# Gate matrices from two float32r products per token, with the gate split into a high and a low part

## The chip, the cores and the metric

The kernel runs on one core of a Trainium2 chip. The metric is device time in microseconds (us), the median of several executions. A core has five engines that run their own instruction queues in order: TensorE (PE, matrix products; its weight loads are shown apart as PEld), VectorE (DVE), ScalarE (ACT), GpSimd (POOL) and SyncE (SP, which only issues transfers here). PE writes its results to a small memory of its own, PSUM, from where DVE or ACT read them.

## What is computed

One residual block over 1024 tokens of width 1024: a normalisation, one input projection, mLSTM heads and gated MLP heads (the "mixers"), an output projection, and then PEER, a layer that picks 16 of 16384 single-neuron experts for each of 8 heads and each token. This last part matters here:

```
s    = scores of a token's query against 2 x 128 keys, per head
s1, i1 = top 16 of the first 128;  s2, i2 = top 16 of the second 128
top_s, pos = top 16 of the 256 sums s1 + s2      -> expert i1 * 128 + i2
gate = softmax(top_s)                            (16 per head, 128 per token)
a    = gelu(x . expert_u[expert])
out  = sum over the token's 128 picks of a * gate * expert_v[expert]
```

## The kernel before

The 1024 tokens are eight blocks of 128. Five blocks (0 to 4) are "dense": all 16384 experts are multiplied out for them, and a gate matrix that is zero for the experts not picked weighs the result. Three blocks (5 to 7) are "sparse": their picked experts are gathered row by row.

The front runs in three parts, with blocks 0 and 1, blocks 2 to 4, and blocks 5 to 7. Each part loads and normalises its tokens, runs the mixers (`head`, `group`), the output projection (products named `po`) and the queries with their scores (`query`: products `pq` and `psc`). Most products there are float32r (`F32R`), three for each pair of matrices, each matrix split into a high and a low part (`mm3`, L94 to L96). After the front come the experts (`experts`): products `pa` and `pout`, while POOL gathers rows for the sparse blocks.

For each dense block, top-k work on DVE (`topk_units`) yields for every token its 128 picks as three rows: first key index, second key index and gate. `done` transposes the three with PE (L483), so that a token is a column, and ACT copies the result to the tile `ijgT` (L485).

`gate_units` then builds the gate matrices in 32 quads of four tokens per block, 160 in all. A token's 128x128 matrix, indexed by the two key indices, is a product of two one-hot matrices over its 128 picks, one of which carries the gates. In a quad, DVE compares a row of the numbers 0 to 127 with both indices of four tokens in one operation (L653, tile `AB`); ACT multiplies one of the one-hots of each token by its gates (L656); PE makes one F32 product per token (L658, tile `pG` in PSUM); ACT copies the four matrices out, transposed, to `Gt` (L659). Every eighth quad a 2 MB piece goes to memory (`d_G`, L661), from where the experts read it (`Gin`, L768). Three buffers of `AB` and two of `pG` bound how many quads are in flight.

The order of instructions on each engine is fixed when the program is built, by a scheduler that follows the program's order. The gate and top-k work of one part's dense blocks is handed out among the next part's work: `interleave` calls the next of these pieces as the main work's given costs (28 for a head, 12 for a group, and so on) add up, and all of them are handed out by a total of 210 out of some 330. So the quads of blocks 0 and 1 stand in the second part's mixers and output projection, and those of blocks 2 to 4 in the third part's. The sparse part has no quads. Operations under `self.first()` (PSUM evictions of the main work) take precedence in that order.

Of the kernel before, what the change touches and what calls it, by code (L numbers as in the profile page):

```python
# [7 lines left out]
F32 = mybir.dt.float32  # L8
F32R = mybir.dt.float32r
# [3 lines left out]
AF = mybir.ActivationFunctionType  # L13
OP = mybir.AluOpType
# [23 lines left out]
NAB = 3  # L38
# [8 lines left out]
class Build:  # L47
# [402 lines left out]
    def topk_units(self, blk):  # L450
        nc, v, tk = self.nc, self.nc.vector, self.tk
# [26 lines left out]
        def done():  # L478
            ijg = st["ijg"]
            if blk in self.dense:  # L480
                pt = self.gps.tile([128, 3, 128], F32, name="pG", tag="pG", bufs=2)
                for k in range(3):
                    nc.tensor.transpose(pt[:, k], ijg[:, k], self.ident)  # L483
                t = self.gp.tile([128, 3, 128], F32, name="ijgT", tag="ijgT", bufs=1)
                nc.scalar.activation(t, pt, AF.Copy)  # L485
                self.pick[blk] = t

        L = []
        for h0 in range(0, 8, HB):
# [149 lines left out]
    def gate_units(self, blk):  # L639
        nc = self.nc  # L640
        pool = self.gp
        s = self.dense.index(blk)
        st = {}

        def quad(tt, q):
            t3 = self.pick[blk]
            if q == 0:
                st["G"] = pool.tile([128, NEXP, TG], F32, name="Gt", tag="Gt", bufs=2)
            Gt = st["G"]
            pg = self.gps.tile([128, 4, 128], F32, name="pG", tag="pG", bufs=2)  # L650
            AB = pool.tile([128, 2, 4, 128], F32, name="AB", tag="AB", bufs=NAB)
            t0 = tt * TG + q * 4
            nc.vector.tensor_tensor(AB, self.iota[:, None, None, :].to_broadcast([128, 2, 4, 128]),  # L653
                                    t3[:, 0:2, t0:t0 + 4, None].to_broadcast([128, 2, 4, 128]), op=OP.is_equal)
            for u in range(4):
                nc.scalar.activation(AB[:, 1, u], AB[:, 1, u], AF.Copy, scale=t3[:, 2, t0 + u:t0 + u + 1])  # L656
            for u in range(4):
                nc.tensor.matmul(pg[:, u], AB[:, 1, u], AB[:, 0, u], start=True, stop=True)  # L658
            nc.scalar.activation(Gt[:, :, q * 4:q * 4 + 4], pg.rearrange("p q i -> p i q"), AF.Copy)  # L659
            if q == TG // 4 - 1:  # L660
                nc.scalar.dma_start(self.d_G[s * (128 // TG) + tt], Gt)  # L661

        return [lambda tt=tt, q=q: quad(tt, q) for tt in range(128 // TG) for q in range(TG // 4)]

    def row(self, pool):

        self.nrow += 1
        if self.dense_phase and self.nrow % (NAB + NGAT) < NAB:
            return self.gp.tile([128, D], F32, name="gat", tag="AB", bufs=NAB)
        return pool.tile([128, D], F32, name="gat", tag="gat", bufs=NGAT)  # L670
# [325 lines left out]
```

## Time and profile before

| | |
|---|---|
| time, median of 3 runs | 2878.07 us (2872.08 to 2878.95) |
| the profiled execution's own time | 2855.23 us |
| its span, first to last instruction | 2853.5 us |
| busy: PE, DVE, POOL, ACT | 94%, 77%, 54%, 39% of the span |
| mean granted clock of TensorE | 0.977 of 2.4 GHz |

The profile is of one execution. "Busy" is the time in which an engine worked on an instruction. A row of a group names the line of the kernel, the engine, the operation, what it writes and reads, its shape (partitions x elements) and how often it ran, and behind the bar the busy time in us, the mean duration of one in ns, and how long the engine stood idle just before, with what ended that. float32r operands of a matrix product are shown as f32. The chain of waits is the work that ended last, followed back from the end to what released each step.

### The profile page before, as it was taken

To read this page: it belongs to the slowest core of one execution; us is meant where nothing else is said; L and a number is where in the kernel's file an instruction comes from. 1 tells how busy PE (TensorE), PEld (TensorE's weight loads), DVE (VectorE), ACT (ScalarE), POOL (GpSimd) and SP (SyncE) were. 2 spreads that over 40 slices of the span, in tenths; PEclk is the share of its full clock that TensorE was granted. 3 is DMA by queue.
4 is the path that set the end of the run, shared out by engine and by line. 5 is a ranking of instruction groups with operands and counts; after the bars stand their busy time and mean duration, and the time that the engine had idled before them with its cause. 6 is when DMAs were issued, how large, how long until landed. Compare 5 with 4: busy or idle time off the path is not lost.

```text
span 2853.5 us, 44691 instructions
## 1 busy us (share of the span) xinstructions
PE 2687.1 (94%) x16223; PEld 2457.0 (86%) x16223; DVE 2195.5 (77%) x4979; ACT 1119.8 (39%) x2293; POOL 1529.3 (54%) x1256
## 2 busy tenths in 40 slices
PE   7888999899899799999999999999999999999998
PEld 6787988889789798889888898889888899889987
DVE  6638985189985777888898788978987777777774
ACT  5444798347888432222222232223222222222222
POOL 4531120001100187767767687767767777777873
PEclk9899999999999899999999999999999999999999
DMA  7788657875669798989989999898889999999992
GB/s 262 238 304 298 228 192 288 275 251 204 228 234 308 278 326 308 325 307 330 332 290 336 339 329 331 309 346 309 316 283 326 356 324 330 346 328 325 338 338 98
DMA packets 329278, 842.63 MB, mean 295 GB/s; under 512 B 25929, under 2 KB 161505, under 8 KB 317281
## 3 DMA queue, kind: packets, MB, share of 16 engines
q0 software_dynamic: 115456, 432.07, 41.2%
q1 hardware_dynamic: 190544, 347.91, 36.8%
q10 hardware_dynamic: 23056, 59.81, 5.5%
q8 instruction: 127, 2.08, 0.3%
q14 instruction: 95, 0.77, 0.1%
HBM read 750.52 MB, written 89.16 MB: 294 GB/s over the span
## 4 chain that ended last, share of the span: by engine, by line
PE 56%; DVE 20%; DMA 10%; issue 5%; ACT 5%; POOL 3%; SPq 1%; ACTq 0%; POOLq 0%; DVEq 0%
PE pout L94 7%; PE pout L96 7%; PE pa L96 7%; PE pout L95 7%; PE pa L94 7%; PE pa L95 7%; PE pG L658 3%; DVE gat L694 2%; DMA Gin<-d_G 2%; DVE sacc L710 2%; DMA gat<-v,ix 2%; DVE AB L653 2%; PE pq L94 2%; PE pq L96 2%; PE pq L95 2%
## 5 line engine op out<-in xcount | busy, mean ns | idle before, releaser
L94 PE MATMUL pa<-xh,uhi 128*128 128x320 f32 x2048 | 637.0, 311 | 24.5 <-ACT uhi L775 14.1
L95 PE MATMUL pa<-xl,uhi 128*128 128x320 f32 x2048 | 634.8, 310 | 0.0
L96 PE MATMUL pa<-xh,ulo 128*128 128x320 f32 x2048 | 623.5, 310 | 4.0 <-POOL ulo L776 3.7
L710 DVE SCALAR_TENSOR_TENSOR sacc<-gat,aw,sacc 128x1024 f32<-128x1024 f32 x384 | 492.1, 1282 | 38.4 <-DMA gat<-v,ix 35.8
L94 PE MATMUL pout<-vhi,wh 128*128 128x512 f32 x1280 | 502.9, 398 | 19.4 <-ACT wh L787 9.8
L95 PE MATMUL pout<-vlo,wh 128*128 128x512 f32 x1280 | 506.5, 397 | 0.4 <-POOL vlo L799 0.4
L96 PE MATMUL pout<-vhi,wl 128*128 128x512 f32 x1280 | 489.3, 397 | 0.7 <-DVE wl L788 0.7
L706 POOL DMA_INDIRECT gat<-v,ix x384 | 364.6, 950 | 228.5 <-DVE sacc L710 126.2
L690 POOL DMA_INDIRECT gat<-u,ix x384 | 364.7, 950 | 200.5 <-DVE gat L694 106.3
L694 DVE SCALAR_TENSOR_TENSOR gat<-gat,xn 128x1024 f32<-128x1024 f32 x384 | 459.0, 1212 | 16.8 <-DMA gat<-u,ix 16.7
L94 PEld LDWEIGHTS pa<-xh,uhi 128*128 128x128 f32 x2048 | 387.4, 189 | 38.1 <-DVE wl L788 14.7
L96 PEld LDWEIGHTS pa<-xh,ulo 128*128 128x128 f32 x2048 | 383.8, 189 | 11.7 <-POOL ulo L776 7.2
L95 PEld LDWEIGHTS pa<-xl,uhi 128*128 128x128 f32 x2048 | 387.3, 189 | 7.3
L776 POOL TENSOR_TENSOR ulo<-raw,uhi 128x1024 fp32r<-128x1024 f32 x128 | 308.8, 2414 | 140.3 <-ACT uhi L775 138.3
L798 ACT ACTIVATE vhi<-raw 128x1024 fp32r<-128x1024 f32 x128 | 131.7, 1052 | 508.7 <-PE pout L95 414.1
L799 POOL TENSOR_TENSOR vlo<-raw,vhi 128x1024 fp32r<-128x1024 f32 x128 | 308.2, 2418 | 26.0 <-ACT vhi L798 24.5
L813 DVE TENSOR_TENSOR acc<-acc,pout 128x512 f32<-128x512 f32 x320 | 214.2, 682 | 124.5 <-PE pout L96 124.2
L94 PEld LDWEIGHTS pout<-vhi,wh 128*128 128x128 f32 x1280 | 240.6, 188 | 73.6 <-DVE acc L813 12.5
L96 PEld LDWEIGHTS pout<-vhi,wl 128*128 128x128 f32 x1280 | 240.2, 189 | 54.8 <-DVE wl L788 1.6
L95 PEld LDWEIGHTS pout<-vlo,wh 128*128 128x128 f32 x1280 | 241.6, 189 | 50.7 <-POOL vlo L799 0.8
L787 ACT ACTIVATE wh<-pa 128x320 fp32r<-128x320 f32 x256 | 111.8, 437 | 358.9 <-DVE pa L786 358.7
L786 DVE TENSOR_TENSOR pa<-pa,Gin 128x320 f32<-128x320 f32 x256 | 126.6, 494 | 154.0 <-ACT pa L784 115.4
(238 smaller groups left out, 5036.9 us busy)
## 6 DMA issues: line engine op xcount, KB each, us to landing
raw<-uT SPq DMA_DIRECT2D x128, 512.0 KB, 6.0
raw<-v SPq DMA_DIRECT2D x128, 512.0 KB, 4.5
wlo<-d_wl SPq DMA_DIRECT2D x48, 1024.0 KB, 5.6
d_G<-Gt ACTq DMA_DIRECT2D x20, 2048.0 KB, 12.0
Gin<-d_G SPq DMA_DIRECT2D x32, 1280.0 KB, 14.3
wraw<-win SPq DMA_DIRECT2D x72, 512.0 KB, 6.9
d_wl<-wlo POOLq DMA_DIRECT2D x24, 1024.0 KB, 8.8
wraw<-wq SPq DMA_DIRECT2D x48, 512.0 KB, 7.5
```

The costliest lines, as they stand in the source:

```text
L94: te.matmul(ps, lh, rh, start=k == 0, stop=False)
L95: te.matmul(ps, lh, rl, start=False, stop=False)
L96: te.matmul(ps, ll, rh, start=False, stop=k == n - 1)
L690: gd = nc.gpsimd.indirect_dma_start(out=t, out_offset=None, in_=self.I["u"], in_offset=bass.IndirectOffsetOnAxis(ap=st["ix"][:, k:k + 1], ...
L694: v.scalar_tensor_tensor(t, t, 1.0, st["xn"], op0=OP.mult, op1=OP.mult, accum_out=st["a"][:, k:k + 1])
L706: gd = nc.gpsimd.indirect_dma_start(out=t, out_offset=None, in_=self.I["v"], in_offset=bass.IndirectOffsetOnAxis(ap=st["ix"][:, k:k + 1], ...
L710: v.scalar_tensor_tensor(st["acc"], t, st["a"][:, k:k + 1], st["acc"], op0=OP.mult, op1=OP.add)
L776: nc.gpsimd.tensor_tensor(ul, ur, uh.bitcast(F32), op=OP.subtract)
L786: v.tensor_tensor(p3, p3, G[:, s * (n32 // 2):(s + 1) * (n32 // 2), e], op=OP.mult)
L798: nc.scalar.activation(vh, vr, AF.Copy)
L799: nc.gpsimd.tensor_tensor(vl, vr, vh.bitcast(F32), op=OP.subtract)
L813: v.tensor_add(st["acc"][:, s, dl], st["acc"][:, s, dl], po)
```

## The change

The gates of a block are split once, in `done`: a high part `ghi`, rounded to float32r by ACT, and a low part, held as its ratio to the high part (`glo`), by four small DVE operations. In a quad, DVE compares only the first index for four tokens (tile `B`, a new tile in the front's memory pool with three buffers). For each token one more DVE operation compares the second index and multiplies by the high gate, and ACT multiplies its result by the ratio, which gives the low part. Both one-hots are now float32r, and PE adds two float32r products per token, high and low, where it made one F32 product.

```diff
@@ topk_units: done @@
                 t = self.gp.tile([128, 3, 128], F32, name="ijgT", tag="ijgT", bufs=1)
                 nc.scalar.activation(t, pt, AF.Copy)
-                self.pick[blk] = t
+                gh = self.gp.tile([128, 128], F32R, name="ghi", tag="ghi", bufs=1)
+                gl = self.gp.tile([128, 128], F32, name="glo", tag="glo", bufs=1)
+                nc.scalar.activation(gh, pt[:, 2], AF.Copy)
+
+                v.tensor_sub(gl, t[:, 2], gh.bitcast(F32))
+                v.tensor_single_scalar(t[:, 2], gh.bitcast(F32), 1e-30, op=OP.max)
+                v.reciprocal(t[:, 2], t[:, 2])
+                v.tensor_mul(gl, gl, t[:, 2])
+                self.pick[blk] = (t, gh.bitcast(F32), gl)
@@ gate_units: quad @@
-            AB = pool.tile([128, 2, 4, 128], F32, name="AB", tag="AB", bufs=NAB)
+            AB = pool.tile([128, 2, 4, 128], F32R, name="AB", tag="AB", bufs=NAB)
+            B = self.fp.tile([128, 4, 128], F32R, name="B", tag="B", bufs=NAB)
             t0 = tt * TG + q * 4
-            nc.vector.tensor_tensor(AB, self.iota[:, None, None, :].to_broadcast([128, 2, 4, 128]),
-                                    t3[:, 0:2, t0:t0 + 4, None].to_broadcast([128, 2, 4, 128]), op=OP.is_equal)
+            nc.vector.tensor_tensor(B, self.iota[:, None, :].to_broadcast([128, 4, 128]),
+                                    t3[:, 0, t0:t0 + 4, None].to_broadcast([128, 4, 128]), op=OP.is_equal)
             for u in range(4):
-                nc.scalar.activation(AB[:, 1, u], AB[:, 1, u], AF.Copy, scale=t3[:, 2, t0 + u:t0 + u + 1])
+                t = t0 + u
+                nc.vector.tensor_scalar(AB[:, 0, u], self.iota, t3[:, 1, t:t + 1], gh[:, t:t + 1],
+                                        op0=OP.is_equal, op1=OP.mult)
+                nc.scalar.activation(AB[:, 1, u], AB[:, 0, u].bitcast(F32), AF.Copy, scale=gl[:, t:t + 1])
             for u in range(4):
-                nc.tensor.matmul(pg[:, u], AB[:, 1, u], AB[:, 0, u], start=True, stop=True)
+                for k in range(2):
+                    nc.tensor.matmul(pg[:, u], AB[:, k, u], B[:, u], start=k == 0, stop=k == 1)
```

## Rows read from the trace of the kernel before

**Rows 1.** The page: its span, the busy time of each engine with its share of the span and its instructions, and the shares of the lines in the chain of waits.

```profile
span 2853.5 us, 44691 instructions
PE 2687.1 (94%) x16223; PEld 2457.0 (86%) x16223; DVE 2195.5 (77%) x4979; ACT 1119.8 (39%) x2293; POOL 1529.3 (54%) x1256
PE pout L94 7%; PE pout L96 7%; PE pa L96 7%; PE pout L95 7%; PE pa L94 7%; PE pa L95 7%; PE pG L658 3%; DVE gat L694 2%; DMA Gin<-d_G 2%; DVE sacc L710 2%; DMA gat<-v,ix 2%; DVE AB L653 2%; PE pq L94 2%; PE pq L96 2%; PE pq L95 2%
```

**Rows 2.** Busy time of each engine by stage: the stretch, its length, then us of PE, PEld, DVE, ACT and POOL with the number of instructions, the granted clock, and the share and rate of the transfers.

```profile
315.00:430.00 115.00, 106.09 (x836) 101.94 (x834) 104.29 (x287) 101.97 (x285) 22.33 (x26) 1.00 0.56 201
430.00:490.00 60.00, 57.62 (x484) 56.33 (x483) 36.48 (x49) 53.03 (x141) 5.01 (x8) 1.00 0.76 280
490.00:660.00 170.00, 151.98 (x954) 142.54 (x953) 93.40 (x470) 77.49 (x135) 10.44 (x21) 0.96 0.76 262
660.00:820.00 160.00, 142.53 (x1064) 135.89 (x1063) 153.47 (x554) 130.43 (x350) 23.34 (x30) 0.96 0.56 201
820.00:950.00 130.00, 124.28 (x924) 122.98 (x923) 78.40 (x160) 110.63 (x292) 2.86 (x6) 0.99 0.89 314
...
985.00:2853.00 1868.00, 1818.31 (x9984) 1630.90 (x9984) 1489.79 (x2565) 486.83 (x804) 1352.38 (x1040) 0.99 0.90 317
```

**Rows 3.** The same stretches, for the one-hots of the gate quads alone (L653): us of DVE, with the number of instructions.

```profile
315.00:430.00 115.00, 53.00 (x43) 1.00 0.56 201
430.00:490.00 60.00, 26.83 (x21) 1.00 0.76 280
...
660.00:820.00 160.00, 62.12 (x51) 0.96 0.56 201
820.00:950.00 130.00, 55.03 (x46) 0.99 0.89 314
```

**Rows 4.** The chain of waits in 315 to 490 us and in 660 to 950 us: shares of the stretch by engine and line.

```profile
by line: PE pG L658 16.5%; DVE AB L653 15.2%; ACT AB L656 7.9%; PE po L94 6.2%; PE po L96 6.1%; PE po L95 5.9%; DVE cv L287 3.4%; PE pg L94 3.1%; PE pg L96 3.1%; PE pg L95 3.1%; ACT Gt L659 2.9%; issue 1.7%; ACT L399 1.5%; ACT whi L77 1.3%;
...
by line: PE pG L658 15.1%; DVE AB L653 9.3%; ACT AB L656 5.5%; SPq L745 4.4%; DMA kk<-keys 4.0%; PE po L94 3.2%; PE pq L96 3.1%; PE pq L94 3.1%; PE po L95 3.1%; PE po L96 3.1%; PE pq L95 3.0%; DMA xl<-d_xl 2.7%; DMA scb<-d_sc 2.1%; ACT Gt L
```

**Rows 5.** Who waited for whom, in 315 to 490 us and in 660 to 950 us: us in total, how often, the longest.

```profile
DVE AB L653 <- PE pG L658: 11.0, 13, 2.9
...
DVE AB L653 <- PE pG L658: 29.4, 21, 5.6
```

**Rows 6.** Groups of instructions of the gate quads.

```profile
L653 DVE TENSOR_TENSOR AB<-iota,ijgT 128x1024 f32<-128x1024 f32 x160 | 197.0, 1240 | 56.0 <-PE pG L658 40.4 <-ACT sc L443 5.7 <-ACT AB L656 5.2
L658 PE MATMUL pG<-AB 128*128 128x128 f32 x1280 | 183.7, 281 | 16.5 <-ACT AB L656 10.7 <-ACT Gt L659 5.4
...
L659 ACT ACTIVATE Gt<-pG 128x512 f32<-128x512 f32 x160 | 92.4, 586 | 20.1 <-PE pG L658 19.3
```

**Rows 7.** DVE in order of time, from three places: start in us, duration in us (of several in a row, from the first start to the last end), then engine, line, operation, tiles, shape and count.

```profile
345.60 1.21 DVE L653 TENSOR_TENSOR AB<-iota,ijgT 128x1024 f32<-128x1024 f32 x1
346.73 0.54 DVE L291 SCALAR_TENSOR_TENSOR qk<-zz,cv 128x384 f32<-128x384 f32 x1
...
347.27 0.46 DVE L285 TENSOR_SCALAR cv<-zz,convw,convb 128x384 f32<-128x384 f32 x1
347.66 0.28 DVE L551 MAX8 tv<-s 128x8 f32<-128x128 f32 x1
...
404.70 0.86 DVE L405 TENSOR_SCALAR vv<-gu,mv,grr 128x128 f32<-128x128 f32 x3 [1.08 <-POOL grr L63]
```

**Rows 8.** Groups of DVE instructions that are near the added ones in form; the last is an answer for one line, with durations in ns as least, median and most.

```profile
L341 DVE TENSOR_TENSOR wT<-pS,wT 128x128 f32<-128x128 f32 x21 | 5.8, 277 | 0.0
...
L151 DVE TENSOR_SCALAR diag<-ident,rall 128x128 f32<-128x128 f32 x6 | 1.7, 286 | 4.2 <-POOL rall L63 4.2
...
L540 DVE RECIPROCAL gsum<-gsum 128x4 f32<-128x4 f32 x8 | 1.3, 161 | 0.0
...
L813 DVE TENSOR_TENSOR acc<-acc,pout x320: 650/682/690, 1029.5 to 2841.7; 128x512 f32<-128x512 f32 x160
```

**Rows 9.** PE in order of time, from four places: the first products after PE had stood, a quad's gate products, and float32r products of 512 and 320 columns.

```profile
321.63 0.39 PE L94 MATMUL pvo<-whi,ah 128*128 128x256 f32 x1 [0.21 <-DVE zz L282]
...
321.85 0.28 PE L95 MATMUL pvo<-wlo,ah 128*128 128x256 f32 x1
...
321.97 0.29 PE L96 MATMUL pvo<-whi,al 128*128 128x256 f32 x1
...
461.49 1.05 PE L658 MATMUL pG<-AB 128*128 128x128 f32 x8
...
1999.82 0.63 PE L96 MATMUL pout<-vhi,wl 128*128 128x512 f32 x2
...
2000.87 0.31 PE L94 MATMUL pa<-xh,uhi 128*128 128x320 f32 x1
2001.01 0.31 PE L95 MATMUL pa<-xl,uhi 128*128 128x320 f32 x1
```

**Rows 10.** ACT in order of time: a quad's four scalings.

```profile
461.46 1.28 ACT L656 ACTIVATE AB<-AB,ijgT 128x128 f32<-128x128 f32 x4
```

**Rows 11.** The transfers of the gate matrices: their issues (durations of the issue in ns, first and last start in us), and the time to landing of all of them.

```profile
L768 SPq DMA_DIRECT2D Gin<-d_G x32: 377/377/426, 978.1 to 2763.1; - x32
L661 ACTq DMA_DIRECT2D d_G<-Gt x20: 326/327/359, 343.0 to 950.3; - x20
...
DMA to landing us min/median/max: 11.1/13.2/20.7
```

More of the change, by code (lines that the diff above doesn't have):

```diff
@@ L645, in quad @@
         def quad(tt, q):
-            t3 = self.pick[blk]
+            t3, gh, gl = self.pick[blk]
             if q == 0:
```

## The prediction

> **What bounds the kernel now.** I read the page first: TensorE (PE) is busy for 94% of the span, VectorE (DVE) for 77%, and by lines the chain of waits is mostly expert products; the gate product, L658, has 3% of it and its one-hots, L653, 2% [rows 1]. These are averages over unlike stages, so next come the busy times stage by stage [rows 2] and, in the same stretches, those of the gate one-hots alone [rows 3]. The 160 quads of gate work (four tokens each) lie in 315 to 490 and 660 to 950 us and nowhere else: the four stretches hold 161, one of them counted on both sides of a border. The 1868 us of experts hold none, and I take their length as unchanged.
>
> There are two kinds of gate stretch. In the mixers (315 to 430, 660 to 820) DVE works 104.3 of 115 and 153.5 of 160 us, more than PE or about as much: DVE sets the pace, PE and ScalarE (ACT) close behind. Behind the mixers (430 to 490, 820 to 950) PE works 57.6 of 60 and 124.3 of 130 us, ACT 53.0 and 110.6, DVE only 36.5 and 78.4: PE sets it. The chain agrees: in both halves L658 and L653 are its two largest lines, 16.5% and 15.2%, then 15.1% and 9.3% [rows 4]. The waits inside the gate work are small beside this: L653 waits for a buffer that L658 frees for 11.0 and 29.4 us in all, mostly where DVE has time [rows 5]. So the change is priced in the mixers on DVE and behind them on PE.
>
> **Prices now.** Durations on DVE overlap: L653 at 345.60 us takes 1.21, but the next operation starts 1.13 later [rows 7]. The step from start to start is what counts; it is some 0.08 us shorter than the duration. Thus L653 costs DVE 1.13 us a quad. On PE a quad is eight records (an F32 product is two, hence 1280 for 640 tokens [rows 6]) in 1.05 us, the last one 0.275 long: a step of 0.111, or 0.89 us a quad [rows 9]. On ACT it is four scalings in 1.28 us, a step of 0.30, and one copy of some 0.48 [rows 6, 10].
>
> **The change on DVE.** The 1024-wide comparison goes; a 512-wide one (B) and four 128-wide compare-and-multiply operations with two per-partition scalars come.
> - B: the 512-wide two-source row L813 has 682 ns, so a step of 0.60 [rows 8].
> - Compare-and-multiply: the trace has neither this pair of operations nor its float32r output, but L405 is a 128-wide F32 operation with two such scalars. Three of them take 0.86 us, the last one 0.34: a step of 0.26 [rows 7]. From below, L151 with one scalar has 286 ns, a step of 0.21 [rows 8]; from above, I let it cost no more than the 384-wide two-scalar L285, whose next operation starts 0.39 later [rows 7]. I take 0.26, the nearest form.
> - A quad then costs 0.60 + 4 x 0.26 = 1.64 us, 0.51 more than now; 0.31 more (1.44) by the low bound and 1.03 more (2.16) by the high. Over 160 quads that is 82 us more (50 to 165).
> - Each of five blocks adds four DVE operations of 128 columns. Subtract and multiply step at 0.20 as L341 does, the maximum at no more than L151's 0.21 [rows 8]. The reciprocal is seen only 4 wide, at 161 ns [rows 8]; 128 wide it lies between 0.21 and, as the widest operation here, 1.13. With 0.4 a block costs 1.0 us (0.8 to 1.7); four blocks start in the mixers: 4 us.
>
> **On PE.** Four F32 products become eight float32r ones: eight weight loads and eight records, as before. The float32r steps of the trace are 0.12 at 256 columns (321.85 to 321.97), 0.14 to 0.15 at 320 and 0.23 at 512 (0.63 less 0.397) [rows 9]; a straight line through them gives 0.067 at 128. No row shows float32r at 128. What speaks against the line: where PE had stood, the first float32r product kept the second waiting 0.22 us instead of 0.12 [rows 9], so an exposed load costs 0.10 and a product of 0.067 can't cover it. I take 0.10, bounds 0.067 and 0.12 (the 256-wide step, with the same load), and as a rival below the price of an F32 product. A quad: 8 x 0.10 = 0.80, a saving of 0.09 (0.35 by the line, a loss of 0.07 by 0.12).
>
> The Trainium skill speaks against the change here: "TensorE: Matmul & The Clock Gate", under "LDWEIGHTS", has a load last as many cycles of 1.2 GHz as it has columns, 107 ns for 128, and its section on weight-path modes denies FP32 weights the fast load. The exposed 0.10 agrees. By that rule a quad would be 0.86 and the saving 0.03 us, so the total below would be 4 us higher.
>
> **Edits that I cost at nothing.** ACT keeps four scalings and the copy per quad; the product with the small ratio is the same form and now waits for one 128-wide operation instead of the whole comparison. The one more ACT copy per block is hidden where ACT is idle (13 us in 315 to 430 alone). Without that cover it is 5 x 0.3 us. B has three buffers like AB, so the number of quads in flight stays. No DMA is added. The last gate write is issued at 950.3 us, its reader at 978.1, and a write takes 13 us: 15 us of slack [rows 11]; what is late by more delays the first expert tile.
>
> **The sum.** Mixers: 43 + 51 quads x 0.51 = 48, and 4 for the blocks: 52 us more DVE work where DVE idles only 10.7 + 6.5 = 17 us. That idle time is spent on answers from ACT and PE, so I let half of it (9) absorb work: +43. What is queued behind the new operations on DVE are the mixers' own: PSUM reads that free PE's tiles, the convolution and mLSTM steps; PE then waits for those. Behind the mixers: 67 quads x 0.51 = 34 us against 75 us of idle DVE: nothing, but 34 if the queue's order gives no cover. PE there saves 67 x 0.09 = 6 us (23 by the line; 5 lost by 0.12). Sum +43 - 6 = **+37 us**. On the profiled execution's 2855.23 us that is 2892. The three runs have their median, 2878.07, 22.8 us above it; I carry the difference over: **2915 us**. Its own range: with the one-scalar price the mixers give 29 + 4 - 9 - 6 = +18; with a price halfway to the upper bound (0.77 a quad) 72 + 4 - 9 - 6 = +61, plus some 10 of late quads behind the mixers: 2890 to 2950.
>
> **Rivals.**
> - *The narrow float32r product costs as much as an F32 one of its width.* Two records of 0.111, so 0.222 each: a quad goes from 0.89 to 1.78, 142 us over 160 quads. For it: the narrowest float32r product here is 256 wide, and the work of before kept 128-wide products in F32. Against: the straight line, and one record per float32r product. PE idles 8.9 + 2.4 + 17.5 + 5.7 = 34 us in the four stretches, so PE becomes the bound everywhere and the time grows by 108 to 142: about 3000 us. It decides from a step of some 0.15 upwards: the mixers' 26 us of idle PE over 94 quads of eight records are 0.035 a record above 0.111.
> - *The new DVE work is hidden.* From 490 to 660 us DVE works 93.4 of 170. If the queues place enough quads that late, the mixers don't grow: 2878 us within 9. Against: quads are handed out along the mixers and the output projection, and in the trace none runs after 490.
> - *Faster: PE gets its saving and DVE stays cheap.* Place: the stretches behind the mixers. Price: at a step of 0.067 the 67 quads there give 23 us; mixers with the one-scalar price and all 17 us of idle time filled cost 29 + 4 - 17 = 16, and less by what their own PE saving (94 x 0.35 = 33 us) unblocks, half of it say: 2878 - 23 = 2855, and 2862 with a part lost. It decides where DVE's addition per quad is below PE's saving: 0.60 + 4p - 1.13 < 0.35, p below 0.22 us. L405 is above that, L151 just below.
>
> **Chances.** Forecast 0.58: the nearest row prices it. F32 price 0.18. Hidden 0.11. Faster 0.13. Measurable is 0.3%, about 9 us. Of the forecast 0.02 fall within that: faster 0.13, same 0.13, slower 0.74. The range goes from the faster case's 2862 up to 3000, the middle of the F32 case; outside lie half of each, 0.16. Own range of the forecast: 2890 to 2950.
>
> **What the changed profile would show.** Right: the 128-wide DVE row steps at 0.26 (0.34 long) x640, B at 0.60; DVE near 100% through both mixers, which grow by some 17 and 25 us; float32r gate products of about 0.10; 490 to 660 and the experts as long as before. Wrong: a gate-product step of 0.22 or 0.067, compare-and-multiply steps under 0.22 or over 0.33, gate quads running into the query stretch, or experts whose length changed.

## The result, and the profile after

The changed kernel takes 2915.09 us (median of four executions, 2910.56 to 2922.12), the kernel before 2875.82 us on the same chip (four, 2872.08 to 2878.95): a ratio of 1.0137 with a 95% interval of 1.0107 to 1.0168, 39 us slower. A second comparison on another chip, below, gives 1.013. The total is the forecast one. Where it arose is partly another matter.

The page of the changed kernel's profiled execution (2922.12 us) shows the span, the busy times and the shares of the lines in the chain of waits; it answers [rows 1].

```profile
span 2920.4 us, 45328 instructions
PE 2728.7 (93%) x16223; PEld 2490.6 (85%) x16223; DVE 2289.6 (78%) x5639; ACT 1127.5 (39%) x2300; POOL 1525.6 (52%) x1256
PE pout L94 7%; PE pa L96 7%; PE pout L95 7%; PE pout L96 7%; PE pa L94 7%; PE pa L95 7%; DMA Gin<-d_G 3%; DVE gat L707 3%; PE pG L671 2%; DVE AB L666 2%; DVE sacc L723 2%; PE pq L94 1%; PE pq L96 1%; POOL gat L719 1%; PE pq L95 1%
```

DVE works 94 us more than before, with 660 more instructions (four for each of 160 quads, four for each of five blocks). PE executes the same 16223 records and is busy for 42 us longer. Over the whole span no engine looks like a new bound; that is the average again.

The gate work of the same execution, one line or form at a time, answers [rows 6, 8]. In the first four rows the durations are in ns, as least, median and most; the last one is the group of the reciprocal, whose price the trace of before bounded no closer than from 0.21 to 1.13 us.

```profile
L666 DVE TENSOR_SCALAR AB<-iota,ijgT,ghi x640: 331/341/1173, 320.8 to 995.5; 128x128 fp32r<-128x128 f32 x160
L662 DVE TENSOR_TENSOR B<-iota,ijgT x160: 652/685/1287, 318.0 to 994.1; 128x512 fp32r<-128x512 f32 x160
L671 PEld LDWEIGHTS pG<-B,AB x1280: 186/192/351, 321.2 to 1002.0; 128*128 128x128 f32 x183
L671 PE MATMUL pG<-B,AB x1280: 218/274/518, 321.2 to 1002.0; 128*128 128x128 f32 x183
L492 DVE RECIPROCAL ijgT<-ijgT 128x128 f32<-128x128 f32 x5 | 4.7, 944 | 0.0
```

Work on DVE and PE around a few quads, in order of time, answers [rows 7, 9, 10].

```profile
455.67 2.82 PE L671 MATMUL pG<-B,AB 128*128 128x128 f32 x12 [0.33 <-ACT AB L668]
...
459.89 0.41 PE L95 MATMUL po<-wlo,ah 128*128 128x256 f32 x1
460.11 0.41 PE L96 MATMUL po<-whi,al 128*128 128x256 f32 x1
...
461.73 0.69 DVE L662 TENSOR_TENSOR B<-iota,ijgT 128x512 fp32r<-128x512 f32 x1 [1.01 <-PE pG L671]
...
463.59 0.69 DVE L662 TENSOR_TENSOR B<-iota,ijgT 128x512 fp32r<-128x512 f32 x1
464.20 1.11 DVE L666 TENSOR_SCALAR AB<-iota,ijgT,ghi 128x128 fp32r<-128x128 f32 x4
464.40 0.98 PEld L671 LDWEIGHTS pG<-B,AB 128*128 128x128 f32 x8
464.52 1.00 PE L671 MATMUL pG<-B,AB 128*128 128x128 f32 x8
```

On DVE, four compare-and-multiply operations take 1.11 us, the last one 0.34: a step of (1.11 - 0.34) / 3 = 0.26, and the comparison `B` before them 0.61. On PE, eight weight loads (PEld) take 0.98 us, the last one 0.19: a step of (0.98 - 0.19) / 7 = 0.113. The eight products take 1.00 us, the last one 0.274 (the median): a mean step of 0.104. Record by record the second product starts 0.061 us after the first, the others 0.108 to 0.114 after the one before. So a product by itself needs no more than 0.061 us, and from the third on it comes at the pace of the loads. The F32 product had eight records at 0.111, so the gate products cost PE about what they did. The 256-wide products at 459.89 us follow each other by 0.22 instead of the 0.12 of [rows 9]: in these few microseconds PE ran at its lower clock of 1.2 GHz (a mean granted clock of 0.57 over 455 to 463 us). Ahead of them it had run little but gate products and waited for ACT's scalings between them (0.33 us at 455.67). DVE then pays too: at 461.73 `B` had waited 1.01 us for a buffer that the slow products held.

The transfers of the gate matrices answer [rows 11].

```profile
L781 SPq DMA_DIRECT2D Gin<-d_G x32: 377/377/404, 1024.9 to 2830.9; - x32
L674 ACTq DMA_DIRECT2D d_G<-Gt x20: 326/326/359, 359.3 to 1003.0; - x20
```

The last write leaves at 1003.0 and the first read at 1024.9 us, 22 us later (28 before): the gate matrices did not hold up the experts. The front (the span up to the experts, which start about 10 us after that read) is 1035 us long, before 988.

**Stages.** The cleanest pair of profiles comes from the last two runs below (2860.48 us before, 2903.37 after), whose experts are equally long. The front is cut at the same events in both: start (not shown), mixers of blocks 2 to 4, their output projection, their queries (left out, 108.7 and 108.2 us), the mixers of blocks 5 to 7, their output projection, their queries, and last the experts. The columns are those of [rows 2]. First the kernel before:

```profile
253.50:431.70 178.20, 166.53 (x1229) 161.15 (x1229) 163.87 (x582) 136.50 (x345) 29.99 (x39) 0.97 0.61 213
431.70:498.50 66.80, 61.07 (x508) 59.20 (x506) 38.15 (x55) 56.77 (x148) 6.31 (x11) 1.00 0.79 286
...
607.20:775.60 168.40, 154.63 (x1147) 149.93 (x1146) 160.77 (x673) 124.32 (x302) 26.63 (x36) 0.97 0.64 225
775.60:856.80 81.20, 72.86 (x571) 69.45 (x569) 73.13 (x199) 71.23 (x190) 6.95 (x10) 0.98 0.66 241
856.80:989.50 132.70, 114.41 (x785) 113.03 (x784) 80.25 (x284) 86.52 (x221) 0.00 (x0) 0.95 0.82 283
989.50:2858.70 1869.20, 1817.76 (x9984) 1630.27 (x9984) 1493.31 (x2541) 486.05 (x803) 1349.86 (x1040) 0.99 0.90 316
```

Then the changed kernel:

```profile
252.00:431.90 179.90, 164.59 (x1161) 157.89 (x1159) 172.72 (x713) 125.17 (x306) 29.06 (x38) 0.94 0.59 207
431.90:509.50 77.60, 73.86 (x577) 71.08 (x575) 62.18 (x189) 70.77 (x190) 6.42 (x12) 0.96 0.71 257
...
617.70:800.10 182.40, 166.25 (x1147) 157.79 (x1146) 177.98 (x813) 125.33 (x304) 23.95 (x36) 0.92 0.59 208
800.10:895.40 95.30, 82.29 (x581) 79.27 (x580) 88.82 (x324) 74.01 (x195) 6.35 (x10) 0.84 0.58 211
895.40:1031.60 136.20, 116.86 (x775) 115.27 (x773) 96.21 (x416) 85.38 (x216) 0.00 (x1) 0.93 0.78 270
1031.60:2901.60 1870.00, 1822.00 (x9984) 1636.21 (x9984) 1495.21 (x2542) 486.30 (x803) 1350.37 (x1040) 0.99 0.90 316
```

The stages grow by 1.7, 10.8, 14.0, 14.1 and 3.5 us; the start and the first queries are 1.5 and 0.5 us shorter; the sum is 42. The experts differ by 0.8. Beside the lengths, three columns matter. DVE's work grows in every stage that holds gate work. PE is busy for longer in most of them although the products are the same, and the granted clock falls, most in the second output projection (0.98 to 0.84).

The number of one-hot comparisons by stage, first of the kernel before (L653), then of the changed one (L662), tells where the quads lie; it answers [rows 3].

```profile
253.50:431.70 178.20, 52.60 (x43) 0.97 0.61 213
431.70:498.50 66.80, 27.18 (x22) 1.00 0.79 286
```

```profile
252.00:431.90 179.90, 23.37 (x35) 0.94 0.59 207
431.90:509.50 77.60, 19.96 (x29) 0.96 0.71 257
```

Eight quads of the first 64 have moved from the mixers to the output projection. That is why the first mixers hardly grow and their projection does. Of the other 96, each of the three later stages holds 32 in both kernels.

Last, the chain of waits by line over 253 to 989 us of the kernel before, and then over 252 to 1031 us of the changed one; they answer [rows 4].

```profile
by line: PE pG L658 11.5%; DVE AB L653 5.3%; PE pq L94 4.8%; PE pq L96 4.8%; PE pq L95 4.8%; ACT AB L656 4.1%; PE po L94 2.8%; DMA scb<-d_sc 2.8%; PE po L96 2.7%; PE po L95 2.7%; ACT whi L77 2.4%; issue 2.1%; SPq L745 2.1%; PE psc L441 1.9%
```

```profile
by line: PE pG L671 9.2%; DVE AB L666 8.3%; DVE B L662 4.8%; PE pq L96 4.6%; PE pq L94 4.5%; PE pq L95 4.5%; DMA scb<-d_sc 2.8%; PE po L94 2.7%; PE po L96 2.7%; PE po L95 2.6%; ACT AB L668 2.5%; DVE cv L287 2.4%; DVE s L558 2.0%; issue 2.0%
```

The one-hots on DVE go from 5.3% to 8.3 + 4.8 = 13.1% of the chain, from 39 to 102 us. The gate products and ACT's scalings lose shares, from 15.6% to 11.7%.

### The profile page after: what moved, and what is told of

It is laid out like the page before. It is cut to its first block, busy times and chain, and to the rows that moved or that the text cites. A ratio compares the mean times of both kernels' runs of the same rounds, so it can differ in the third digit from the quotient of the medians.

```text
span 2920.4 us, 45328 instructions
## 1 busy us (share of the span) xinstructions
PE 2728.7 (93%) x16223; PEld 2490.6 (85%) x16223; DVE 2289.6 (78%) x5639; ACT 1127.5 (39%) x2300; POOL 1525.6 (52%) x1256
## 4 chain that ended last, share of the span: by engine, by line
PE 51%; DVE 16%; DMA 6%; issue 5%; ACT 4%; POOL 4%; SPq 1%; ACTq 0%; another core or an unknown queue 0%; POOLq 0%; DVEq 0%
PE pout L94 7%; PE pa L96 7%; PE pout L95 7%; PE pout L96 7%; PE pa L94 7%; PE pa L95 7%; DMA Gin<-d_G 3%; DVE gat L707 3%; PE pG L671 2%; DVE AB L666 2%; DVE sacc L723 2%; PE pq L94 1%; PE pq L96 1%; POOL gat L719 1%; PE pq L95 1%
## 5 line engine op out<-in xcount | busy, mean ns | idle before, releaser
L94 PEld LDWEIGHTS pout<-vhi,wh 128*128 128x128 f32 x1280 | 241.4, 189 | 82.0 <-DVE acc L826 16.1
```

What stands on the lines that cost most here:

```text
L94: te.matmul(ps, lh, rh, start=k == 0, stop=False)
```

## The experiments

The theory: the added DVE work, in stages where DVE has little idle time, makes the time. Rivals: the products themselves (their price, or the clock that they leave PE), and a longer wait from one-hot to gate matrix rather than DVE's volume. Each comparison is against the kernel before on the same chip, since that kernel's medians went from 2855 to 2876 us between chips; a range that an expectation gives in absolute time has to be shifted by that. Each variant also gets an instruction order of its own on PE, DVE and ACT, so a part of any difference can be the order's; no run holds the order fixed. A variant that was to move one of the two comparisons to POOL has no measured time. "Front" is again the profiled span up to the experts: 989.5 and 990.9 us in two more profiles of the kernel before, 1031.6 and 1040.7 in two more of the changed one.

**The DVE part alone.** The products stay F32, one per token; DVE and ACT work as in the changed kernel, except for one subtraction fewer per block.

```diff
...
-            AB = pool.tile([128, 2, 4, 128], F32R, name="AB", tag="AB", bufs=NAB)
-            B = self.fp.tile([128, 4, 128], F32R, name="B", tag="B", bufs=NAB)
+            AB = pool.tile([128, 2, 4, 128], F32, name="AB", tag="AB", bufs=NAB)
+            B = self.fp.tile([128, 4, 128], F32, name="B", tag="B", bufs=NAB)
...
-                for k in range(2):
-                    nc.tensor.matmul(pg[:, u], AB[:, k, u], B[:, u], start=k == 0, stop=k == 1)
+                nc.tensor.matmul(pg[:, u], AB[:, 1, u], B[:, u], start=True, stop=True)
```

> The DVE part of the change without its PE part: DVE makes B and the four compare-and-multiply one-hots as the changed kernel does, ACT scales each by the ratio of the full gate to its high part, and PE makes one F32 product per token, as before. Theory (DVE's price sets the time): about the changed kernel's 2915 us, 2900 to 2925, with DVE near 100% busy in both mixers. Rival (the narrow float32r products, or a clock that falls because of them, set it): about the time of before, 2868 to 2885, and the granted clock in the gate stretches back at 0.96 to 1.00 where the changed kernel has 0.87 to 0.96.

Measured: 2912.97 us against 2855.29, 1.0192 [1.0162, 1.0222], within the theory's range and, beside the faster kernel before of this chip, a larger loss than the change's own; the front is 1042.9 us. First output projection, second mixers and second output projection:

```profile
435.40:509.20 73.80, 69.89 (x563) 66.92 (x561) 59.21 (x176) 66.63 (x178) 6.74 (x12) 1.00 0.71 258
...
615.90:802.10 186.20, 165.67 (x1146) 158.25 (x1144) 178.90 (x788) 125.40 (x304) 24.53 (x34) 0.92 0.58 203
802.10:915.20 113.10, 92.22 (x629) 86.42 (x628) 102.49 (x386) 85.25 (x227) 7.02 (x12) 0.89 0.52 198
```

DVE alone makes a front as long as the changed one's, +53 us for 790.1 - 709.4 = 81 us more DVE work. In the second mixers and their projection DVE works 179 of 186 and 102 of 113 us. Note the first row: the granted clock stays at 1.00 with F32 products. In the other two it falls with them too.

**The PE part alone.** DVE and ACT work as before (plus one ACT operation per block), two float32r products per token replace the F32 one.

```diff
+                nc.scalar.activation(t[:, 2], pt[:, 2], AF.Copy, scale=0.5)
...
-            AB = pool.tile([128, 2, 4, 128], F32, name="AB", tag="AB", bufs=NAB)
+            AB = pool.tile([128, 2, 4, 128], F32R, name="AB", tag="AB", bufs=NAB)
...
-                nc.tensor.matmul(pg[:, u], AB[:, 1, u], AB[:, 0, u], start=True, stop=True)
+                for k in range(2):
+                    nc.tensor.matmul(pg[:, u], AB[:, 1, u], AB[:, 0, u], start=k == 0, stop=k == 1)
```

> The PE part without the DVE part: one 1024-wide comparison per quad as before, now in float32r; ACT scales by half the gate; PE adds two float32r products of the same one-hots per token. Only the split is left out (the gates carry float32r precision). Theory (DVE): the time of before, 2867 to 2885; steps of the gate products 0.11 us, bound by the weight load. Rival (narrow products): 2900 to 2920, with a lower granted clock in the gate stretches.

Measured: 2879.21 us against 2855.29, 1.0086 [1.0052, 1.012]. The theory's range held only in absolute time: the loss is 24 us, more than the front explains, which is 996.9 us, 7 more than before. First mixers, first output projection and last queries:

```profile
250.00:425.60 175.60, 166.14 (x1215) 162.35 (x1213) 161.12 (x580) 130.78 (x334) 29.30 (x39) 0.94 0.62 217
425.60:497.70 72.10, 65.98 (x521) 63.23 (x520) 39.38 (x57) 60.81 (x159) 7.26 (x11) 0.95 0.72 266
...
855.50:996.90 141.40, 117.65 (x777) 116.39 (x776) 78.92 (x282) 85.11 (x216) 0.00 (x0) 0.90 0.76 262
```

The products save nothing. The clock is 0.94 where it was 0.97 with PE as busy (166 us of a shorter stage), and 0.95 instead of 1.00 in the projection. The experts took 1874.3 us, and the scheduler had put their instructions into another order; the rest of the 24 us isn't located.

**Half the dose on DVE.** Only two of a quad's four compare-and-multiply operations are made and their results are used twice. A quad costs DVE 0.60 + 2 x 0.256 = 1.11 us, as much as before (1.13).

```diff
-                nc.vector.tensor_scalar(AB[:, 0, u], self.iota, t3[:, 1, t:t + 1], gh[:, t:t + 1],
-                                        op0=OP.is_equal, op1=OP.mult)
-                nc.scalar.activation(AB[:, 1, u], AB[:, 0, u].bitcast(F32), AF.Copy, scale=gl[:, t:t + 1])
+                if u < 2:
+                    nc.vector.tensor_scalar(AB[:, 0, u], self.iota, t3[:, 1, t:t + 1], gh[:, t:t + 1],
+                                            op0=OP.is_equal, op1=OP.mult)
+                nc.scalar.activation(AB[:, 1, u], AB[:, 0, u % 2].bitcast(F32), AF.Copy, scale=gl[:, t:t + 1])
...
-                    nc.tensor.matmul(pg[:, u], AB[:, k, u], B[:, u], start=k == 0, stop=k == 1)
+                    nc.tensor.matmul(pg[:, u], AB[:, k, u if k else u % 2], B[:, u], start=k == 0, stop=k == 1)
```

> The changed kernel with compare-and-multiply for two of a quad's four tokens; the other two tokens use the first two's high one-hots, so their gates are wrong and part of the work is left out. DVE works 0.60 + 2 x 0.26 = 1.12 us a quad, as before; PE, ACT and the waits stay those of the changed kernel. Theory (DVE): back near the time of before, 2870 to 2890. Rival (PE or clock): still 2905 to 2920. Rival (the finer chain from DVE over ACT to PE, whatever its price): in between, 2890 to 2905.

Measured: 2885.93 us against 2855.29, 1.0111 [1.0076, 1.0145]: 31 us above before, so in between, as the second rival had it, and within the theory's range only in absolute time. The front is 1004.3 us with 717.5 us of DVE (before: 709.4). Both mixers, each followed by its output projection:

```profile
251.80:422.90 171.10, 162.15 (x1160) 156.67 (x1158) 154.89 (x651) 119.58 (x301) 25.79 (x38) 0.94 0.60 216
422.90:500.70 77.80, 72.89 (x574) 70.53 (x575) 47.57 (x124) 71.13 (x191) 6.24 (x12) 0.95 0.73 261
...
608.60:774.90 166.30, 155.77 (x1148) 150.60 (x1146) 159.91 (x715) 123.74 (x302) 23.82 (x34) 0.97 0.63 224
774.90:867.60 92.70, 81.79 (x562) 79.10 (x561) 76.29 (x295) 72.44 (x192) 7.10 (x12) 0.81 0.60 219
```

With DVE's volume nearly back to its old size the front is 27 to 36 us shorter than in the changed kernel, but still 15 longer than before. Half of these 15 the products alone gave. The others, some 7 us, are left for the finer chain of one comparison, two compare-and-multiply steps, four scalings and eight products; the last stage shown is 11.5 us longer than before at a granted clock of 0.81. Whether the chain lowers the clock or the clock stretches the chain, these runs don't separate.

The stages say where DVE's volume counts. The quads lie as in the changed kernel (35, 29, 32, 32, 32). From half to full dose the two mixers grow by 8.8 and 16.1 us for 36 us of DVE work, but the two projections by -0.2 and 2.6 us for 27, and the last queries not at all. So the mixers are where the volume costs time; most of what the projections lost against the kernel before (10.8 and 14.1 us) is there at half dose already.

**Both kernels again, twice.** In the first pair of profiles the changed kernel's experts were longer too; these runs ask whether the change does that.

> The changed kernel once more, beside the next run, to split its loss between the front and the experts on one chip. In the first two profiles the front (up to the first expert product) grew from 988.5 to 1035.0 us and the experts from 1865 to 1885 us. Theory (the change costs the front alone; the experts' 20 us are another chip or execution): front 1030 to 1040, experts within 6 us of the next run's. Rival (the change lengthens the experts too): experts 12 us or more longer than the next run's.

> The kernel before once more, for a profile on the same chip: front 985 to 992 us, experts 1860 to 1885 us.

> A third profile of the changed kernel, for the length of the experts, which were 1885 us in both earlier profiles against 1865 and 1867 before, while the timed medians (2915 less a front of 1035 to 1041; 2868 and 2876 less 990) leave 1873 to 1885 us for both kernels. Theory (the experts' length varies with the execution, not with the change): within 8 us of the next run's, or on the other side. Rival (the change lengthens the experts): again 15 us or more longer than the next run's. The front: 1033 to 1042 us either way.

> A third profile of the kernel before, the partner of the run above: front 985 to 993 us; experts 1860 to 1890.

Measured: the changed kernel 2915.67 us against 2868.29, 1.013 [1.0082, 1.0178]; the single profiled runs 2927.66 and 2859.74, then 2903.37 and 2860.48. The fronts are 1040.7 and 990.9, then 1031.6 and 989.5 us; the experts 1885.2 and 1867.1, then 1870.0 and 1869.2. So the front grows by 50 and 42 us; the experts' 18 us (20 in the very first pair, 1885 against 1865) are gone in the last pair, with the same two programs. The rival's sign came in one pair and the theory's in the next: the experts vary from run to run in a way that these profiles don't explain, and their length is no part of what the change is shown to do.

**One product instead of two.** The changed kernel with the small part's product alone; the high part's is left out. PE's gate work is halved, DVE's is kept.

```diff
-                for k in range(2):
-                    nc.tensor.matmul(pg[:, u], AB[:, k, u], B[:, u], start=k == 0, stop=k == 1)
+                nc.tensor.matmul(pg[:, u], AB[:, 1, u], B[:, u], start=True, stop=True)
```

> The changed kernel with the low product alone: the high product is left out, so the gate matrices are wrong; DVE, ACT and the chain from DVE over ACT to PE stay, PE's gate work is halved (4 instead of 8 loads and products of 0.11 us, 0.45 us a quad, 71 us in all). Theory (DVE's price sets the mixers, PE the stretches behind them): 5 to 30 us faster than the changed kernel, still slower than before. Rival (the narrow products set the time): 40 us or more faster, at or below the time of before.

**One float32r product on the kernel before.** The same halving where DVE has its old work. The gate and its one-hot are rounded to float32r, so this one is less exact.

```diff
-            AB = pool.tile([128, 2, 4, 128], F32, name="AB", tag="AB", bufs=NAB)
+            AB = pool.tile([128, 2, 4, 128], F32R, name="AB", tag="AB", bufs=NAB)
...
-                nc.scalar.activation(AB[:, 1, u], AB[:, 1, u], AF.Copy, scale=t3[:, 2, t0 + u:t0 + u + 1])
+                nc.scalar.activation(AB[:, 1, u], AB[:, 1, u].bitcast(F32), AF.Copy, scale=t3[:, 2, t0 + u:t0 + u + 1])
```

> A version from the finding that a 128-wide float32r record costs as much as one of the two records of an F32 product: the kernel before with float32r one-hots and one product per token, so that PE's gate work is halved (0.45 instead of 0.89 us a quad, 71 us in all). The gates then carry float32r precision and not F32; nothing else is left out. Theory (DVE sets the mixers, PE and ACT the stretches behind them): the front 0 to 15 us shorter, for the mixers stay as they are and the clock falls where PE idles. Rival (PE sets the front): 30 us or more shorter.

Measured, first one: 2933.74 us against 2868.29, 1.0225 [1.0185, 1.0264], 18 us more than the changed kernel on the same chip, where 5 to 30 us less were expected: both expectations missed. Measured, second one: 2862.53 against 2870.54, 0.9974 [0.9953, 0.9996], a little faster than the kernel before; its front is 26 us shorter, between the theory's 15 and the rival's 30. Front and experts of the first:

```profile
0.00:1036.10 1036.10, 865.05 (x5600) 808.62 (x5600) 784.59 (x3038) 636.55 (x1496) 174.03 (x216) 0.88 0.70 243
1036.10:2930.80 1894.70, 1825.67 (x9984) 1637.04 (x9984) 1516.59 (x2601) 490.06 (x805) 1352.93 (x1040) 0.98 0.89 312
```

and of the second:

```profile
0.00:963.40 963.40, 828.63 (x5599) 781.10 (x5599) 698.78 (x2378) 629.79 (x1489) 178.77 (x216) 0.91 0.75 260
963.40:2856.10 1892.70, 1829.54 (x9984) 1639.68 (x9984) 1510.57 (x2601) 486.96 (x803) 1349.96 (x1040) 0.98 0.90 313
```

Both drop 640 records, worth 640 x 0.112 = 72 us at full clock, and PE's work falls by 42 or 43 (from 907.5 and 871.8), while the granted clock falls as well (0.91 to 0.88, 0.95 to 0.91). With the old DVE work the front gets 26 us shorter (9 in the two mixers, 11 in the last queries), with the new one 5 at most (its first queries, with four quads moved there, are 11 us longer). So PE looks like the nearer bound in the kernel before, and with the new DVE work relief of PE helps little. Both also moved 60 DVE instructions from the front to the experts (x2601 instead of x2541), and both have experts of 1893 to 1895 us, which takes most of the second one's gain back. That the moved instructions cause it is likely, not shown; of the 18 us by which the first is slower, the profiles explain only the experts' part.

**Twice the dose.** Every compare-and-multiply is made twice.

```diff
-                nc.vector.tensor_scalar(AB[:, 0, u], self.iota, t3[:, 1, t:t + 1], gh[:, t:t + 1],
-                                        op0=OP.is_equal, op1=OP.mult)
+                for _ in range(2):
+                    nc.vector.tensor_scalar(AB[:, 0, u], self.iota, t3[:, 1, t:t + 1], gh[:, t:t + 1],
+                                            op0=OP.is_equal, op1=OP.mult)
```

> The changed kernel with each compare-and-multiply made twice: DVE works 0.60 + 8 x 0.26 = 2.68 us a quad, 1.04 more, 166 us more in all; PE, ACT and the waits stay. From half to full dose the front grew by 37 us (1004 to 1041) for 83 us of DVE work, a slope of 0.45. Theory (DVE's price sets the front, and more so the fuller DVE is): front 1130 to 1200 us, the time 90 to 160 us above the changed kernel's. Rival (the queues' order hides the rest behind the mixers, or another engine sets the pace): less than 60 us above it.

Measured: 3053.33 us against 2870.54, 1.0624 [1.057, 1.0678]; that is 138 us above the changed kernel's 2915.67, within the theory's 90 to 160. The front is 1126.5 us, just under the theory's range and 86 to 95 more than the changed kernel's, for 940.9 - 796.4 = 145 us more DVE work in the front. The rest lies in the experts, which took 1925.8 us here, with 92 DVE instructions moved there from the front (x2634). Both mixers and the second output projection:

```profile
254.90:453.00 198.10, 175.15 (x1139) 166.78 (x1139) 195.69 (x809) 120.98 (x291) 23.86 (x36) 0.85 0.51 179
...
654.90:869.30 214.40, 174.23 (x1148) 166.25 (x1146) 212.61 (x921) 130.25 (x305) 25.41 (x34) 0.84 0.51 178
869.30:986.30 117.00, 94.62 (x565) 88.20 (x564) 117.00 (x467) 73.97 (x186) 8.97 (x12) 0.74 0.47 174
```

Here DVE is busy for 99 to 100% of all three stages. From dose to dose the front answers to DVE's volume with a rising slope: from half to full dose 27 to 36 us for 77 to 79 of work (0.35 to 0.46), from full to double 86 to 95 for 145 (0.59 to 0.65).

**Cheaper one-hots on the kernel before.** One comparison in bfloat16 on DVE, POOL copies the unscaled one-hots to F32, ACT scales the others out of bfloat16.

```diff
...
-            nc.vector.tensor_tensor(AB, self.iota[:, None, None, :].to_broadcast([128, 2, 4, 128]),
-                                    t3[:, 0:2, t0:t0 + 4, None].to_broadcast([128, 2, 4, 128]), op=OP.is_equal)
+            oh = self.fp.tile([128, 2, 128, 4], BF, name="ohg", tag="ohg", bufs=NAB)
+            nc.vector.tensor_tensor(oh, self.iota4[:, None].to_broadcast([128, 2, 128, 4]),
+                                    tb[:, :, None, t0:t0 + 4].to_broadcast([128, 2, 128, 4]), op=OP.is_equal)
+            nc.gpsimd.tensor_copy(AB[:, 0], oh[:, 0].rearrange("p i u -> p u i"))
             for u in range(4):
-                nc.scalar.activation(AB[:, 1, u], AB[:, 1, u], AF.Copy, scale=t3[:, 2, t0 + u:t0 + u + 1])
+                nc.scalar.activation(AB[:, 1, u], oh[:, 1, :, u], AF.Copy, scale=t3[:, 2, t0 + u:t0 + u + 1])
```

> A version from the theory: the kernel before, with both comparisons in one 1024-wide bfloat16 operation (exact for numbers to 127; the trace's L528 and L532 have 0.60 us a step at that size, against 1.13 in F32), POOL widening one half to F32 (1 to 1.5 us a quad on an engine that is idle there), ACT scaling the other from bfloat16 into F32; PE keeps the F32 products. Theory (DVE sets the mixers): 10 to 40 us faster than before. Rival (ACT and PE are as close a bound): within 9 us of before. Rival (POOL's copy comes late or slows DVE): slower than before.

Measured: 2874.31 us against 2868.29, 1.0018 [0.9993, 1.0042], no difference, as the first rival had it. The comparison fell from 1.24 to 0.69 us and the front's DVE work from 709 to 651 us, but the front stays at 989.4. The first output projection:

```profile
421.30:495.50 74.20, 68.77 (x576) 67.21 (x577) 35.59 (x64) 70.06 (x187) 28.29 (x43) 1.00 0.72 267
```

So 58 us less of DVE work bring nothing, while 85 to 87 more cost 42 to 50: in the kernel before, DVE sets the pace at most jointly with PE and ACT. A part of the gain may also be lost to this variant's own chain: from the mixers of blocks 2 to 4 to the experts, DVE's comparison waits 78.6 us for a buffer that ACT's scalings still read; before, it waited 46.3 us for PE's products and 5.2 for ACT.

**The same with float32r and POOL scaling.** One float32r product as above, and two of the four scalings of a quad on POOL.

```diff
...
-                nc.scalar.activation(AB[:, 1, u], oh[:, 1, :, u], AF.Copy, scale=t3[:, 2, t0 + u:t0 + u + 1])
+                g1 = t3[:, 2, t0 + u:t0 + u + 1]
+                if u < 2:
+                    nc.gpsimd.tensor_scalar(AB[:, 1, u], oh[:, 1, :, u], g1, None, op0=OP.mult)
+                else:
+                    nc.scalar.activation(AB[:, 1, u], oh[:, 1, :, u], AF.Copy, scale=g1)
```

> All three engines relieved at once: bfloat16 comparison (DVE 0.60 us a quad), POOL widening one half (0.66 us) and scaling two of four tokens, ACT scaling two (1.1 instead of 1.65 us a quad), one float32r product per token (PE 0.45 us a quad); the gates carry float32r precision. Theory (three engines stand close together before, so relief of one gives nothing and relief of all gives time): the front 20 to 50 us shorter than before's 990. Rival (the main work's own chain sets the front): within 10 us of it.

Measured: 2972.55 us against 2870.54, 1.0334 [1.0261, 1.0407]; the front is 1029.9 us, 40 longer than before, and both expectations missed. The last queries:

```profile
867.40:1029.90 162.50, 120.10 (x704) 115.35 (x704) 82.41 (x314) 82.27 (x189) 91.90 (x135) 0.80 0.65 225
```

POOL's scaling takes 0.62 us in the median, twice over and with a copy of 0.65 per quad. POOL, which had nothing to do in this stage, works 92 us, and the stage is 30 us longer than before. That POOL makes the quads late is likely, not shown: over the whole run, engines stood idle for 83.9 us before an instruction on `AB` until one of POOL's scalings was done. The experts grew to 1944.7 us, for a reason that isn't settled.

## Why the prediction was right, and where it was not

**DVE's prices: right.** Compare-and-multiply steps at 0.256 us (taken 0.26, from the nearest form in [rows 7]) and `B` at 0.61 (0.60). The front's DVE work grew by 85 to 88 us in three pairs of profiles, against 82 + 5. Only the reciprocal was mis-sized: it lasts 0.944 us, a step of some 0.86 instead of 0.4, towards the upper bound, worth 0.5 us a block.

**PE's price: wrong, and harmless.** The term "8 x 0.10 = 0.80, a saving of 0.09" measured 8 x 0.113 = 0.90 by the loads against 0.89: no saving, and the 6 us behind the mixers were not there. The exposed load of 0.10 was the right thing to look at, but it was too short: the loads step by 0.113 us, while the product alone needs no more than 0.061, below even the straight line's 0.067. The Trainium skill, "TensorE: Matmul & The Clock Gate", section "LDWEIGHTS", gives a load of P columns about P / 1.2 ns, which is 107 for 128; the trace's 113 is nearer to that than to the 100 that I took. The rival of an F32-priced product (0.222) is excluded by the same rows.

**The mixers: right in mechanism, wrong in place.** The sum put 17 us into the first mixers and 25 into 660 to 820 us. Measured: +1.7 in the first mixers and +10.8 in their projection, because eight of 43 quads moved on to it. The step assumed that quads stay in their stage. By halves it fits better, 12.5 against 17, and 28.1 for the second mixers and projection together, but only as a number: by the half dose 8.8 and 16.1 us in the mixers are DVE's volume, and the projections grew mostly for other reasons. The reading that DVE alone sets the pace in the mixers of the kernel before was too strong: cheaper one-hots took 58 us off DVE's front and left its length (989.4 us).

**Behind the mixers: the step that failed.** "67 quads x 0.51 = 34 us against 75 us of idle DVE: nothing" was wrong. The projections grew by 10.8 and 14.1 us. Of the 75 idle microseconds 23.5 were in the first projection and 44 in the queries (855 to 950 us has 51.0 of 95). The second projection had next to none. Cut at its real borders (775.6 and 856.8 us) it has 73.1 of 81.2 us of DVE work already, so the 32 x 0.51 = 16 us had 8 to hide in. Its first 45 us, in which DVE works 44.95, my border at 820 us had counted with the mixers; its last part I had added to the queries. But missing cover is the smaller part of it: at half dose, with 76 of 92.7 us of DVE, the stage is 11.5 us longer already, and two float32r products alone give 3. The rest goes with the finer chain and the lower clock, which no run separates. In the first projection DVE still had 29 us free, and it grew by 11 all the same. Here PE sets the length (73.9 of 77.6 us), and what it got is seven more quads. With F32 products and the same 29 quads the stage is 73.8 and 74.2 us long, whether DVE works 59 us (the DVE part alone) or 36 (cheaper one-hots): some 7 us go with the quads that moved. With float32r products, at 0.95 to 0.96 of the clock, it is 77.6 to 77.8, some 4 us more, at full and at half dose alike (82.6 in one more profile of the changed kernel, at 0.92). In the last queries the cover was real: 16 us more work, +3.5.

**Why the total came out.** +25 us that were not forecast in the projections, +3.5 in the queries, and no saving, stand against 27 us less than forecast in the mixers (15.7 instead of 43). The 42 to 50 us of the front agree with +37 in size, and half of DVE's added work on the path was the right share overall; a good part of that agreement is luck between terms. That the median meets 2915 us to the microsecond is chance too: the second comparison gave +47 us, and the kernel before alone moved by 20 us between chips. By the experiments some 27 to 36 us are DVE's volume, 25 of them in the mixers, and some 7 the products with their lower clock, while the last 7 or so are put down to the finer chain, by subtraction only. The parts don't add up: DVE alone gives 53, and the PE part on top of it does not lengthen the front (1031.6 to 1040.7 against 1042.9); each variant's own order of instructions may hide behind that.

**Rivals.** "Hidden" holds for the queries alone. "Faster" needed a pace of 0.067 for the products and a DVE step under 0.22; neither was there. The experts' length is unchanged in the last pair, as assumed; their scatter of 15 us between profiles of one program was not on my list.

## What to carry to other kernels

Cut a profile at the events of the program (the last mixer, the first query), not at round times: a stage whose engine is 90% busy can vanish in the mean with an idle neighbour. Where several engines are almost equally busy, relief of one may bring nothing while an addition to the same one still costs: here 58 us less on DVE brought nothing and 43 less on PE brought 26 us of the front, while 85 to 87 more on DVE cost 42 to 50. And the cost appears where a fixed order has pushed the work, so a stage can grow on another engine than the one that was changed. A 128-wide float32r product with new weights is paid by its weight load (0.113 against 0.061 us), so splitting one F32 product into two float32r ones of that width moved no time off TensorE.

## What was not expected of the hardware

- Two narrow float32r products (128 columns) take about as long as one F32 product: two loads at 0.113 = 0.226 us against two records at 0.111 = 0.222 us per token.
- The granted clock is lower with them in some stages at a like busy share of PE: 1.00 in the first output projection with F32 products (before, and with the DVE part alone), 0.95 and 0.96 with float32r ones. In the second mixers the PE part alone hardly shows it (0.97 and 0.96). In the second projection both parts count: 0.98 before, 0.94 with the PE part alone, 0.89 with the DVE part alone, 0.84 with both. What lowers it is not shown: a busy share is itself raised by a lower clock, so equal shares don't mean equal work. At the lower clock a narrow float32r record takes twice its step, some 0.22 us (twelve in 2.82 us).
- A 128-wide reciprocal on DVE takes 944 ns, more than the comparison of four tokens at once (685).
- The experts of one and the same program took 1870.0 and 1885.2 us in two profiles.
